# Two of four output blocks as seven block products, with their weight sums formed in DRAM

## The chip, the core and the metric

The kernel runs on one core of a Trainium2 chip. The metric is the device time of one execution in microseconds (us). Before the change the median of three runs is 1606.47 us (1606.38 to 1606.73). The core's engines work side by side: TensorE (PE) multiplies matrices, VectorE (DVE) and ScalarE (ACT) do elementwise work, GpSimd (POOL) a few small operations and accumulating DMA transfers, and SyncE (SP) issues the loads of the weights.

## The reference

One layer of a decoder trunk works on 256 rows of 2048 channels in float32: a normalisation, one wide projection `w_in`, a sparse attention branch and a retention branch, a gated merge of both, an output projection, and a squared-ReLU feed-forward part. What the change touches is the merge and what follows it:

```python
merged = jax.nn.sigmoid(ga) * (o_attn @ w_up_attn[l]) + jax.nn.sigmoid(gb) * (o_ret @ w_up_ret[l])
x = x + merged @ w_out[l]
h2 = rms_norm(x, ln2_g[l])
x = x + jnp.square(jax.nn.relu(h2 @ w_ff1[l])) @ w_ff2[l]
```

`merged`, `w_out`: 256 x 2048 and 2048 x 2048.

## The kernel before, in words

**Matmuls.** Each float32 operand is split into a rounded part hi and a rest lo, and a product is three matmuls, hi·hi, hi·lo and lo·hi (`products`, L434), of 128 x 128 stationary activations by 128 x 512 weights. The 256 rows are two row tiles t; the 2048 input channels are 16 k-chunks of 128. A *block* is 512 output columns: 16 chunks, 2 row tiles, 3 matmuls. The output projection has four blocks O0 to O3, the retention branch's projection UR0 to UR3, and the first group of the feed-forward part F1(1) and F1(0), in this order.

**Weights.** A load brings four chunks (1 MB) from DRAM into one of four buffers `raw` (L325 to L333) over SP's queue. Two chunks at a time, an *item*, are split: ScalarE writes `whi` (L379), VectorE `wlo` (L380). `program` (L150) lists all items in order; `ahead` (L397) issues loads up to 8 items and splits 2 items (3 from the feed-forward pools on) ahead of their use. Three pairs of split buffers go round, a fourth joins where the pool `f1` or `fourth` is there.

**Block products.** In the gates and in the later feed-forward groups two blocks together (2048 x 1024 weights, quarters A to D) are made by Strassen's scheme in Winograd's form: seven products of 8 chunks for one row tile each, in the order `ORDER`, in place of eight (`strassen`, L695). Some products use sums of quarters; VectorE adds those in the weight buffers (L367), and a few are added by an accumulating DMA of POOL into a buffer (L387). The products' banks are combined by VectorE (L712 to L724), with copies of three banks on ScalarE (L716). The activations need four differences (G3, G5, G6, G7) beside the plain quarters.

**Who sets the order.** The program text gives each instruction a place; a planner then places the instructions of each engine by a simulated time at which they are ready and, among those ready, by place. `tc.high_priority(offset=60)` puts an instruction 60 places ahead; in the gate stage the splits and the bank sums have it. Helpers such as norms and transposes are generators in a list `work`, advanced one `yield` by each `step()`, which is called once or twice per item.

**Around the change.** After UR0 and UR1, `merge` (L948) forms the merged rows on VectorE, `merged_in` (L944) transposes them on TensorE into a bank of the pool `pt` and splits them into `mT`. PSUM's eight banks are dealt as `pm` 4, `pt` 2, `pa` 2 there. After UR3 a `drain()` (L970) finishes all helpers. Then come O0 to O3 (L1029): each adds its bank into `x2` (L1033), squares it on ScalarE with a row sum (L1035) and writes it out to `sums`. After O2 the root of the mean square of three blocks is formed (L1040 to L1042, the power on POOL, L450), and the columns 0, 1 and 2 are normalised by it during O3 (`next_norm`, L988: a scaled copy L993, transposes L1001, a copy by the gain L1003, the split into `xf` L985 and L986). Column 3 follows in F1(1), with the differences for the block products (`forms`, L1009); a later factor makes up for the root of three blocks alone. F1(1) reads its chunks in the order of columns 0, 1, 2, 3.

Of the kernel before, what the change touches and what calls it, by code (L numbers as in the profile page):

```python
# [17 lines left out]
P = 128  # L18
# [60 lines left out]
def stream():  # L79
# [22 lines left out]
    b += [(("O", i), "w_out", 0, DK, i * BN, BN) for i in range(4)]  # L102
# [28 lines left out]
def block(key):  # L131

    return [(key, h, s) for h in range(DK // KC) for s in range(KC // HC)]
# [16 lines left out]
def program():  # L150
# [8 lines left out]
    for key in [("UR", 2), ("UR", 3)] + [("O", i) for i in range(4)] + [("F1", i) for i in (1, 0)]:  # L159
        out += block(key)  # L160
# [20 lines left out]
def block_kernel(ctx, tc, cst, rot, xt, gains, w, x, ret_gn_g, ret_gn_b, out):  # L181
# [89 lines left out]
    at, B, off = {}, {}, 0  # L271
    for key, name, _, nk, _, n in stream():
        B[key] = (nk, n)
        for h in range(nk // KC):
            src = w[off:off + KC * P * n].rearrange("(p c n) -> p c n", p=P, c=KC)
            if key in BESIDE:
# [5 lines left out]
    use = program()  # L282

    def tile_of(item):
        if item[0] == "Q":
# [5 lines left out]
    def sum_of(item):  # L291

        if item[0] == "Q":
# [57 lines left out]

    def split(i):
        if first_gate - 16 <= i <= last_gate:
# [43 lines left out]
    def ahead(i):  # L397
        for _ in range(2):
# [16 lines left out]
    def run_blocks(keys, act, before=None):  # L415
# [3 lines left out]
        for k0 in range(0, nk, HC):  # L419
            for key, p in zip(keys, ps):  # L420
                n = B[key][1]
                ws = weights((key, k0 // KC, k0 % KC // HC))
                for c in range(HC):
# [4 lines left out]
                    products(p, [z[:, c, :n] for z in ws], [act(k, t) for t in range(T)], k == 0, k == nk - 1)  # L428
        return [[z[:, :B[key][1]] for z in p] for key, p in zip(keys, ps)]

    def run_block(key, act, before=None):
        return run_blocks([key], act, before)[0]
# [262 lines left out]
    def strassen(item):  # L695
# [4 lines left out]
        p = ORDER[n]  # L700
# [12 lines left out]
        with tc.high_priority(offset=AHEAD) if u in GATES else nullcontext():  # L713
# [230 lines left out]
    def merged_in(i, t, m):  # L944
        yield from transpose_in(mT, 4 * i, t, m)
# [11 lines left out]
    for i in range(2):  # L957
        merge(i, both_ps[i])
    work.append(branches(2))
    for i in (2, 3):  # L960
        ps = run_block(("UR", i), of(rT))
        if i == 2:
            drain()
        merge(i, ps)
# [5 lines left out]
    drain()  # L970
    ex.release()
# [3 lines left out]
    late["f2"] = ctx.enter_context(tc.tile_pool(name="f2", bufs=1, side="right", reuse_waits="tile"))  # L975
# [3 lines left out]
    xf = late["f1"].tile([P, 2, len(PRODUCTS), HK, P], F32R, tag="xf", name="xf")  # L979
    xr = [late["f2"].tile([P, T, HK, P], F32, tag="rawb", name=nm("xr"), bufs=2) for _ in range(2)]  # L980
# [48 lines left out]
    for i in range(4):  # L1029
        ps = run_block(("O", i), of(mT))  # L1030
        for t in range(T):
            z = x2[:, t, i * BN:(i + 1) * BN]
            nc.vector.tensor_tensor(z, ps[t], z, op=ALU.add)  # L1033
            junk = stage()
            nc.scalar.activation(junk, z, AF.Square, accum_out=ss2[:, 4 * t + i:4 * t + i + 1])  # L1035
            nc.scalar.dma_start(sums[:, t, i * BN:(i + 1) * BN], z)
        if i == 2:

            ss = small(T)
            nc.vector.tensor_reduce(ss, ss2.rearrange("p (t i) -> p t i", t=T)[:, :, :3], axis=AX.X, op=ALU.add)  # L1040
            rs = cp.tile([P, T], F32, name="rs")
            nc.vector.tensor_copy(rs, rsqrt(ss, T, 1.0 / (3 * BN)))  # L1042
            work.append(z for k in range(3) for z in next_norm(k))
# [4 lines left out]
    def norm_end():  # L1048
        yield from next_norm(3)
# [24 lines left out]
    for i in (1, 0):  # L1074
        ps = run_block(("F1", i), lambda k, t: form(quads[k // HK][t], k % HK))
# [87 lines left out]
```

## Time and profile before

| what | us |
|---|---|
| median of three runs | 1606.47 |
| the profiled execution | 1606.29 |
| its span, first to last instruction | 1604.3 |
| TensorE busy in it | 1597.7 |
| VectorE busy | 1298.9 |
| ScalarE busy | 1017.4 |
| GpSimd busy | 126.5 |

In the rows of the profile, a line such as L380 is a line of the kernel, `out<-in` are the program's buffers, `xN` is a count. A row of instructions in order of time has the start, the busy time, the engine, the line and, in brackets, how long the engine stood idle ahead of it and who released it. A row of a stage has its bounds and length, then the busy time and number of instructions of TensorE, of its weight loads, of VectorE, ScalarE and GpSimd, then TensorE's granted clock, the busy share of the DMA engines and GB/s. A row of a group has the busy time, the mean in ns, and the idle time ahead. A row of waits has the total, the number and the longest. A row of transfers has the number, the size and the median time from issue to landing.

### The profile page before, as it was taken

Reading aid. Unit: us, or ns where it says so; the run is one execution under the profiler, and the core shown is the slowest. Engines: PE = TensorE matmul, PEld = TensorE weight load, DVE = VectorE, ACT = ScalarE, POOL = GpSimd, SP = SyncE. Lnnn points to the kernel's source line nnn. Section 1 sums busy time; section 2 is a strip of 40 time slices with the busy share of each in tenths; the row PEclk is TensorE's granted clock in tenths of the full one; section 3 lists DMA queues with packets and bytes.
Section 4 is the critical chain, followed back from the end, with each engine's and each line's share of the span. In section 5 each row is a group of like instructions: output and inputs, shape, how many; then the busy total and the mean of one; then the engine's idle time right before and its main releaser. Section 6 shows DMA issues by size and latency. Waiting matters only on the chain.

```text
span 1604.3 us, 19728 instructions
## 1 busy us (share of the span) xinstructions
PE 1597.7 (100%) x7394; PEld 1327.8 (83%) x7394; DVE 1298.9 (81%) x1354; ACT 1017.4 (63%) x1262; POOL 126.5 (8%) x169
## 2 busy tenths in 40 slices
PE   9999999999999999999999999999999999999998
PEld 8978888888888888888888888888888888888887
DVE  6578777998989899677765579898989898989884
ACT  7555567666766666454444666767767776767672
POOL 0000001010000001112210000000000000000000
PEclk9999999999999999999999999999999999999999
DMA  9645348978878684765766574767676767777673
GB/s 331 220 146 186 135 153 305 299 266 274 258 287 266 230 258 176 285 222 195 265 250 250 194 277 149 257 194 246 204 260 200 242 213 236 236 236 236 216 205 130
DMA packets 75759, 368.57 MB, mean 230 GB/s; under 512 B 8592, under 2 KB 15376, under 8 KB 42512
## 3 DMA queue, kind: packets, MB, share of 16 engines
q1 hardware_dynamic: 56224, 311.32, 53.0%
q0 software_dynamic: 16704, 49.82, 14.3%
q10 hardware_dynamic: 2736, 6.18, 1.0%
q8 instruction: 58, 0.95, 0.2%
q14 instruction: 37, 0.30, 0.1%
HBM read 337.92 MB, written 29.36 MB: 229 GB/s over the span
## 4 chain that ended last, share of the span: by engine, by line
PE 97%; DVE 2%; ACT 0%; issue 0%; DVEq 0%
PE pm L439 14%; PE pm L440 14%; PE pm L438 14%; PE pq L438 9%; PE pq L439 9%; PE pq L440 9%; PE pf L438 7%; PE pf L439 7%; PE pf L440 7%; PE pt L467 1%; DVE wlo L380 1%; DVE mid L593 1%; PE pa L438 0%; PE pa L439 0%; PE pa L440 0%; PE pa L264 0%
## 5 line engine op out<-in xcount | busy, mean ns | idle before, releaser
L380 DVE TENSOR_TENSOR wlo<-raw,whi 128x1024 fp32r<-128x1024 f32 (+2 forms) x556 | 659.7, 1200 | 206.1 <-ACT whi L379 197.9
L379 ACT ACTIVATE whi<-raw 128x1024 fp32r<-128x1024 f32 (+2 forms) x556 | 576.0, 1043 | 382.3 <-PE pm L440 233.9
L438 PE MATMUL pm<-whi,act 128*128 128x512 f32 (+1 forms) x992 | 384.7, 388 | 0.0
L439 PE MATMUL pm<-wlo,act 128*128 128x512 f32 (+1 forms) x992 | 381.8, 385 | 0.5 <-DVE wlo L380 0.5
L440 PE MATMUL pm<-whi,act 128*128 128x512 f32 (+1 forms) x992 | 381.4, 384 | 0.0
L380 DVE TENSOR_TENSOR wlo<-rawc,whi 128x1024 fp32r<-128x1024 f32 x176 | 214.7, 1220 | 42.2 <-ACT whi L379 40.4
L379 ACT ACTIVATE whi<-rawc 128x1024 fp32r<-128x1024 f32 x176 | 186.6, 1060 | 85.7 <-PE pf L440 23.2
L439 PEld LDWEIGHTS pm<-wlo,act 128*128 128x128 f32 x992 | 186.4, 188 | 35.9 <-DVE wlo L380 3.0
L440 PEld LDWEIGHTS pm<-whi,act 128*128 128x128 f32 x992 | 186.2, 188 | 35.1
L438 PEld LDWEIGHTS pm<-whi,act 128*128 128x128 f32 x992 | 186.4, 188 | 33.9 <-issue 0.3
L438 PE MATMUL pf<-whi,act 128*128 128x512 f32 x512 | 200.0, 391 | 0.0
L439 PE MATMUL pf<-wlo,act 128*128 128x512 f32 x512 | 199.4, 390 | 0.0
L440 PE MATMUL pf<-whi,act 128*128 128x512 f32 x512 | 199.4, 389 | 0.0
L367 DVE TENSOR_TENSOR raw<-raw,raw 128x2048 f32<-128x2048 f32 x86 | 196.6, 2286 | 0.8
L438 PE MATMUL pq<-whi,xf 128*128 128x512 f32 x392 | 154.3, 394 | 0.0
L439 PE MATMUL pq<-wlo,xf 128*128 128x512 f32 x392 | 152.8, 390 | 0.0
L440 PE MATMUL pq<-whi,xf 128*128 128x512 f32 x392 | 152.8, 390 | 0.0
L440 PEld LDWEIGHTS pf<-whi,act 128*128 128x128 f32 x512 | 96.1, 188 | 20.1
L438 PEld LDWEIGHTS pf<-whi,act 128*128 128x128 f32 x512 | 96.0, 188 | 20.1 <-ACT whi L379 0.4
L439 PEld LDWEIGHTS pf<-wlo,act 128*128 128x128 f32 x512 | 96.1, 188 | 19.7
L1109 POOL DMA_DIRECT2D sums<-ev x56 | 49.1, 969 | 580.8 <-ACT ev L1108 579.9
L440 PEld LDWEIGHTS pq<-whi,xf 128*128 128x128 f32 x392 | 73.6, 188 | 15.3
(206 smaller groups left out, 1623.2 us busy)
## 6 DMA issues: line engine op xcount, KB each, us to landing
raw<-in_w_dram SPq DMA_DIRECT2D x188, 1024.0 KB, 6.1
rawc<-in_w_dram SPq DMA_DIRECT2D x56, 1024.0 KB, 6.3
rawc<-in_w_dram SPq DMA_DIRECT2D x64, 512.0 KB, 5.9
sums<-ev POOLq DMA_DIRECT2D x56, 256.0 KB, 5.5
raw<-in_w_dram POOLq DMA_DIRECT2D x10, 1024.0 KB, 9.9
raw<-in_w_dram SPq DMA_DIRECT2D x8, 736.0 KB, 5.0
raw<-in_w_dram SPq DMA_DIRECT2D x7, 512.0 KB, 7.9
raw<-in_w_dram SPq DMA_DIRECT2D x8, 368.0 KB, 7.8
```

What stands on the lines that cost most here:

```text
L367: nc.vector.tensor_tensor(one, one, two, op=ALU.add)
L379: nc.scalar.activation(a, src, AF.Copy)
L380: nc.vector.tensor_tensor(b, src, a.bitcast(F32), op=ALU.subtract)
L438: nc.tensor.matmul(d, h, hi, start=first, stop=False, skip_group_check=skip)
L439: nc.tensor.matmul(d, h, lo, start=False, stop=False, skip_group_check=skip)
L440: nc.tensor.matmul(d, l, hi, start=False, stop=last, skip_group_check=skip)
L467: nc.tensor.transpose(ps[:, c * P:(c + 1) * P], src[:, c * P:(c + 1) * P], ident)
L593: nc.vector.scalar_tensor_tensor(sc[t], src, iw[:, t, h:h + 1], sc[t], op0=ALU.mult, op1=ALU.add)
L1109: nc.gpsimd.dma_start(sums[:, t, i * BN:(i + 1) * BN], z, accum_op=ALU.add)
```

## The change

The blocks O0 and O1 become one pair of block products, `OUT = ("O", 0)`, in the order X11 A, G7 B, X12 D, G5 A, G3 C, G6 C, X22 D. The sums of weight quarters that they need are formed in DRAM tiles `pre`: eight plain copies of 1 MB by SP at items 24 to 45, and eight accumulating transfers by POOL at items 46 to 73, all in the index and attention projections. The products' 14 loads and those of O2 and O3 go through the four `raw` buffers. The items of the first two products stand between those of UR3; then come four items of O2, and then the remaining 20 product items with the other 12 of O2 and O3 between them, the last of those ahead of the last three product items.

The splits of the stretch and the bank sums of `OUT` get the 60 places. `merged_in` also copies the transposed rows to `xr`, and a new helper `m_forms` makes the four differences. The banks are dealt as `pm` 4, `pq` 3, `pt` 1 right after UR0 and UR1; the drain after UR3 goes. The root for the norm is formed from the columns 2 and 1 alone, once both are complete; these two are normalised first, then 3 and 0, and F1(1) takes its chunks in that order.

```diff
+OUT = ("O", 0)
+OUT_ORDER = (0, 2, 5, 1, 3, 4, 6)
+NORM_COLS = (2, 1, 3, 0)
...
+def second_half():
+    q = [("Q", OUT, n, h, s) for n in range(len(OUT_ORDER)) for h in range(HK // KC) for s in range(KC // HC)]
+    a, b = q[:8], q[8:]
+    out = block(("UR", 2))
+    for x, y in zip(block(("UR", 3)), a):
+        out += [x, y]
+    two = block(("O", 2)) + block(("O", 3))
+    out, two = out + two[:4], two[4:]
+    n, j = len(b) - 2, 0
+    for i, x in enumerate(b):
+        out.append(x)
+        while j < len(two) and j * n < (i + 1) * len(two):
+            out.append(two[j])
+            j += 1
+    return out
...
+    pre = {z: dp.tile([HK // KC, P, KC * BN + 16], F32, name=nm("pre"))[:, :, :KC * BN].rearrange("h p (c n) -> h p c n", c=KC) for z in QUARTERS}
+    for n, p in enumerate(OUT_ORDER):
+        z = PRODUCTS[p][1]
+        for h in range(HK // KC):
+            at[("OQ", n), h] = (pre[z][h] if p in (1, 2, 4, 6) else base[z, h], BN)
+    background = {}
+    for j, (z, two) in enumerate((("A", "B"), ("B", "C"), ("C", "A"), ("D", "C"))):
+        for h in range(HK // KC):
+            background[24 + 6 * j + 3 * h] = (pre[z][h], base[z, h], False)
+            background[46 + 8 * j + 3 * h] = (pre[z][h], base[two, h] if j < 2 else pre[two][h], True)
...
     def split(i):
-        if first_gate - 16 <= i <= last_gate:
+        if first_gate - 16 <= i <= last_gate or first_out - 4 <= i <= last_out:
             with tc.high_priority(offset=AHEAD):
...
     def ahead(i):
+        if i in background:
+            d, a, add = background[i]
+            if add:
+                nc.gpsimd.dma_start(d, a, accum_op=ALU.add)
+            else:
+                nc.sync.dma_start(d, a)
...
-        with tc.high_priority(offset=AHEAD) if u in GATES else nullcontext():
+        with tc.high_priority(offset=AHEAD) if u in GATES or u == OUT else nullcontext():
...
     def merged_in(i, t, m):
...
+        split_into(mT, 4 * i, 4, t, ps)
+        half, c0 = divmod(4 * i, HK)
+        nc.scalar.activation(xr[half][:, t, c0:c0 + 4, :], ps.rearrange("p (c i) -> p c i", c=4), AF.Copy)
         moved[0] += 1
...
+    deal(pm=4, pq=3, pt=1)
...
+    def m_forms():
+        while moved[0] < 2 * T:
+            yield
+        for c in (0, 4):
...
+            nc.vector.tensor_tensor(d, xr[0][:, 1, c:c + 4, :], xr[0][:, 0, c:c + 4, :], op=ALU.subtract)
+            nc.scalar.activation(hi, d, AF.Copy)
...
+            nc.vector.tensor_tensor(lo, d, hi.bitcast(F32), op=ALU.subtract)
...
+        for f, d, one, two in ((G5, x22, x21, x22), (G6, x11, x11, x22), (G3, x12, x12, x11)):
...
+    def out_block(i, t, src):
+        z = x2[:, t, i * BN:(i + 1) * BN]
+        nc.vector.tensor_tensor(z, src, z, op=ALU.add)
+        junk = stage()
+        nc.scalar.activation(junk, z, AF.Square, accum_out=ss2[:, 4 * t + i:4 * t + i + 1])
+        nc.scalar.dma_start(sums[:, t, i * BN:(i + 1) * BN], z)
+        done.add((i, t))
...
-    drain()
-    ex.release()
...
+    def first_norms():
+        lo, n = min(NORM_COLS[:2]), 2
+        ss = small(T)
+        nc.vector.tensor_reduce(ss, ss2.rearrange("p (t i) -> p t i", t=T)[:, :, lo:lo + n], axis=AX.X, op=ALU.add)
+        nc.vector.tensor_copy(rs, rsqrt(ss, T, 1.0 / (n * BN)))
+        for k in NORM_COLS[:2]:
+            yield from next_norm(k)
...
+        if not started and all((i, t) in done for i in NORM_COLS[:2] for t in range(T)):
+            started = True
+            work.append(first_norms())
     drain()
...
-        yield from next_norm(3)
+        for k in NORM_COLS[2:]:
+            yield from next_norm(k)
...
-        ps = run_block(("F1", i), lambda k, t: form(quads[k // HK][t], k % HK))
+        ps = run_block(("F1", i), lambda k, t: form(quads[k // HK][t], k % HK), order=NORM_COLS if i else range(DK // KC))
```

More of the change, by code (lines that the diff above doesn't have):

```diff
@@ L699, in strassen @@
         b, e = blocks[u]["b"], blocks[u]["e"]
-        p = ORDER[n]
+        p = product_of(u, n)
         ws = weights(item)
@@ new lines, in m_forms @@
+    def m_forms():
+        while moved[0] < 2 * T:
+            yield
+        for c in (0, 4):
+            z = stage()
+            d = z.rearrange("p (c i) -> p c i", c=4)
+            hi, lo = m7[c // KC] = [sp.tile([P, KC, P], F32R, tag="stg", name=nm("stg"), bufs=n_stg) for _ in range(2)]
+            nc.vector.tensor_tensor(d, xr[0][:, 1, c:c + 4, :], xr[0][:, 0, c:c + 4, :], op=ALU.subtract)
+            nc.scalar.activation(hi, d, AF.Copy)
+            yield
+            nc.vector.tensor_tensor(lo, d, hi.bitcast(F32), op=ALU.subtract)
+            yield
+        while moved[0] < 4 * T:
+            yield
+        (x11, x21), (x12, x22) = ([z[:, t] for t in range(T)] for z in xr)
+        for f, d, one, two in ((G5, x22, x21, x22), (G6, x11, x11, x22), (G3, x12, x12, x11)):
+            hi, lo = (mx["xf"][:, a, f] for a in range(2))
+            nc.vector.tensor_tensor(d, one, two, op=ALU.subtract)
+            nc.scalar.activation(hi, d, AF.Copy)
+            yield
+            nc.vector.tensor_tensor(lo, d, hi.bitcast(F32), op=ALU.subtract)
+            formed.add(f)
+            yield
@@ new lines, in plain @@
+    def plain(item, act):
+        (key, i), h, s = item
+        ws = weights(item)
+        if (h, s) == (0, 0):
+            acc[key, i] = [psum("pm") for _ in range(T)]
+        for c in range(HC):
+            step()
+            k = h * KC + s * HC + c
+            products(acc[key, i], [z[:, c] for z in ws], [act(k, t) for t in range(T)], k == 0, k == DK - 1)
+        return acc.pop((key, i)) if k == DK - 1 else None
+    done = set()
+    def out_block(i, t, src):
[5 more added lines that the diff above has]
+        done.add((i, t))
@@ new lines, in block_kernel @@
+    work.append(branches(2))
+    work.append(m_forms())
+    blocks[OUT] = {"form": m_form, "finish": lambda u, t, i, dst, src: out_block(i, t, src), "b": {}, "e": {}}
+    rest = second_half()
+    while rest[0][0] != ("O", 2):
+        item = rest.pop(0)
+        if item[0] == "Q":
+            strassen(item)
+            continue
+        ps = plain(item, of(rT))
+        if ps:
+            if item[0][1] == 2:
+                while moved[0] < T * 2 or any(z.gi_frame is not None and z.__name__ == "branches" for z in work):
+                    step()
+            merge(item[0][1], ps)
@@ L1027, in forms @@
         late["g7"] = xr[0][:, 1:2]
[L1029 to L1043, printed above, removed]
+    rs = cp.tile([P, T], F32, name="rs")
+    def first_norms():
[5 more added lines that the diff above has]
+            yield from next_norm(k)
+    started = False
+    while rest:
+        item = rest.pop(0)
+        if item[0] == "Q":
+            strassen(item)
+        else:
+            ps = plain(item, of(mT))
+            for t in range(T if ps else 0):
+                out_block(item[0][1], t, ps[t])
+        if not started and all((i, t) in done for i in NORM_COLS[:2] for t in range(T)):
+            started = True
+            work.append(first_norms())
     drain()
```

65 lines of the change are left out of this document (43 added, 22 removed).

## The prediction

> **What bounds the kernel now.** I read the page first, for busy times and for the chain that ended last.
>
> ```profile
> PE 1597.7 (100%) x7394; PEld 1327.8 (83%) x7394; DVE 1298.9 (81%) x1354; ACT 1017.4 (63%) x1262; POOL 126.5 (8%) x169
> ...
> PE 97%; DVE 2%; ACT 0%; issue 0%; DVEq 0%
> ```
>
> A busy TensorE need not be a TensorE at its peak, since ends are modelled. So the second view is the list of what TensorE waited for, and the third its instructions one by one in a plain output block (the first and the last of 54 matmuls).
>
> ```profile
> PE pa L264 <- DVE warm L259: 1.1, 1, 1.1
> PE pq L438 <- ACT mid L676: 0.9, 1, 0.9
> PE pm L439 <- DVE wlo L380: 0.5, 2, 0.3
> ```
> ```profile
> 879.82 0.39 PE L439 MATMUL pm<-wlo,act 128*128 128x512 f32 x1
> ...
> 891.83 0.39 PE L438 MATMUL pm<-whi,act 128*128 128x512 f32 x1
> ```
>
> TensorE waits 2.5 us in the whole run, and one matmul of 512 columns follows the other every (891.83 - 879.82) / 53 = 0.2266 us. The kernel is bound by its number of matmuls: one less is worth 0.2266 us, as long as nothing new makes TensorE wait. All the rest of the argument is about new waits. The profiled execution took 1606.29 us (span 1604.3 and 2.0 around it), 0.18 under the median 1606.47 of the three runs; the sum is made on 1606.29, and 0.18 is added at the end.
>
> **Matmuls removed.** Two plain output blocks are 2 x 16 k-chunks x 2 row tiles x 3 = 192 matmuls. Seven products of 8 k-chunks x 3 are 168. The transposes keep their number. 24 x 0.2266 = **-5.44 us**. This is all that can be won.
>
> **Splits, forms, bank sums and copies added.** 28 weight splits stand in place of 16, and there are four differences of activations with their splits, five bank sums, three bank copies and eight copies of transposed rows. These rows give what the engines do now from the third UR block to late in the last O block, in the gate stage (which already runs such products beside plain blocks), in the 22 us in which three columns are normalised, and in the 22 us at the start of the output blocks; then the price of one split (VectorE's half) and of one sum.
>
> ```profile
> 812.00:924.00 112.00, 112.00 (x514) 92.59 (x513) 63.19 (x67) 58.91 (x81) 0.72 (x1) 1.00 0.61 223
> 250.00:500.00 250.00, 250.00 (x1103) 206.29 (x1102) 224.09 (x188) 173.61 (x192) 22.62 (x37) 1.00 0.84 284
> 902.00:924.00 22.00, 22.00 (x109) 18.04 (x108) 12.70 (x17) 18.48 (x33) 0.72 (x1) 1.00 0.47 161
> 836.00:858.00 22.00, 22.00 (x100) 18.30 (x100) 13.36 (x14) 9.84 (x11) 0.00 (x0) 1.00 0.81 319
> ```
> ```profile
> L380 DVE TENSOR_TENSOR wlo<-raw,whi 128x1024 fp32r<-128x1024 f32 (+2 forms) x556 | 659.7, 1200 | 206.1 <-ACT whi L379 197.9
> ```
> ```profile
> 333.43 0.68 DVE L712 TENSOR_TENSOR stg<-pq,stg 128x512 f32<-128x512 f32 x1
> ...
> 335.17 1.29 DVE L712 TENSOR_TENSOR stg<-stg,stg 128x512 f32<-128x512 f32 x2
> 336.37 0.68 DVE L712 TENSOR_TENSOR stg<-pq,stg 128x512 f32<-128x512 f32 x1
> 336.97 1.21 DVE L380 TENSOR_TENSOR wlo<-raw,whi 128x1024 fp32r<-128x1024 f32 x1
> ...
> 344.85 0.74 DVE L785 SCALAR_TENSOR_TENSOR stg<-stg,r,stg 128x512 f32<-128x512 f32 x1
> ```
>
> VectorE gets 12 x 1.20 for splits, four ops of 0.68 and six of about 1.2 for the differences, and 5 x 0.68 for sums: 14.4 + 10 + 3.4 = 28. 63 + 28 = 91 us of 112 - 5 = 107, or 85%. The gate stage has 224 / 250 = 90% and TensorE waits nowhere in it. ScalarE gets 12 x 1.04 (a row of its own chain further down), and eleven copies and five activation splits between 0.6 and 1.05, some 11 us: 59 + 24 = 83 of 107, or 77%; the row at 902 has 18.5 / 22 = 84%, again without a wait. So this work costs 0, its cover being matmuls at a load that other stages carry. Its upper end is 1 us, about the one wait of 0.9 above.
>
> **One transpose bank where there were two.** A bank of transposed rows is read by three operations, hi, lo and the new copy, 0.6 to 0.7 each. Were two sets of transposes queued back to back on the one bank, TensorE, in order, would stand about 1.9 us, and all matmuls behind it; four such pairs are 7.6. The feed-forward stage has the same deal of banks:
>
> ```profile
> 1114.47 0.49 PE pt L467 x4
> 1117.04 0.44 PE pt L467 x4
> ```
>
> There the two sets stand 2.6 us apart, matmuls between them, with no entry in the list of waits. I take 0 of the range 0 to 7.6. The drain after the last UR block goes too; its transposes are covered by the four items of O2 that follow, 48 x 0.2266 = 10.9 us.
>
> **The memory sums.** Eight plain copies of 1 MB stand in SP's queue ahead of weight loads, and eight accumulating transfers in POOL's, between some 60 and 190 us. No row has a transfer from memory to memory; the nearest are weight loads of 1 MB in that stretch and the gate stage's accumulation into a buffer (POOL's queue); the third row is SP's longest wait, that for a split to free a buffer.
>
> ```profile
> raw<-in_w_dram SPq DMA_DIRECT2D x10, 1024.0 KB, 4.8
> ```
> ```profile
> raw<-in_w_dram POOLq DMA_DIRECT2D x7, 1024.0 KB, 10.2
> ```
> ```profile
> SPq L333 <- DVE wlo L380: 1091.5, 239, 16.1
> ```
>
> So one is 4.8 to 10.2 us of transfer. There are four weight buffers, and a plain block uses up one in 24 x 0.2266 = 5.44 us; a load that finds one copy ahead lands 10 to 15 us after its issue, against three further buffers, 16.3 us. It fits: 0. Two transfers ahead of one load would miss by up to 4.8 + 2 x 10.2 - 16.3 = 9 us: the upper end, and a rival below. Behind a POOL transfer stands only the small power of a norm in that stretch, about an issue (0.5 to 1 us) late.
>
> **The norm behind the output blocks: where I expect the loss.** Now the root of three blocks' squares is formed while the fourth block (96 matmuls, 21.8 us) runs. These rows, VectorE's and then ScalarE's in order of time, are the chain from the last matmul of the third block.
>
> ```profile
> 899.71 1.28 DVE L1033 TENSOR_TENSOR x<-pm,x 128x512 f32<-128x512 f32 x2
> ...
> 902.51 0.16 DVE L1040 TENSOR_REDUCE small<-ss 128x2 f32<-128x6 f32 x1
> ...
> 903.71 0.17 DVE L1042 COPY rs<-small 128x2 f32<-128x2 f32 x1 [0.84 <-POOL small L450]
> ...
> 908.81 1.29 DVE L986 TENSOR_TENSOR xf<-xr,xf 128x512 fp32r<-128x512 f32 x2 [1.35 <-ACT xf L985]
> ...
> 914.44 1.29 DVE L986 TENSOR_TENSOR xf<-xr,xf 128x512 fp32r<-128x512 f32 x2
> ```
> ```profile
> 903.91 1.34 ACT L993 ACTIVATE stg<-x,rs 128x512 f32<-128x512 f32 x2 [1.44 <-DVE rs L1042]
> 905.16 1.04 ACT L379 ACTIVATE whi<-raw 128x1024 fp32r<-128x1024 f32 x1
> 906.11 1.54 ACT L1003 ACTIVATE xr<-pt,gT 128x256 f32<-128x256 f32 x4
> ```
>
> From the block's end to the first half column that a matmul can use (908.81 + 0.68) it is 9.8 us, with 12 us to spare. After the change the root needs columns 2 and 1, and column 1 is complete with product G6 C, the sixth. Behind that stand four items of the seventh product (6 matmuls each) and two of O3 (12 each): 48 x 0.2266 = 10.9 us, and the first column's own eight transposes, some 0.9 (four took 0.44 above). Cover: **11.8 us**. Then F1 needs column 2 and TensorE has nothing else to do.
>
> The chain gets longer. Ahead of it come four bank sums, 0.60 apart: 2.4. They and the splits up to the last product are 60 places ahead in priority, the adds into x2 are not, so the second add can fall behind the splits of the next three items, 3 x 1.14 = 3.4; the gate rows show it happen, the sums until 336.97 and the ordinary operation behind them at 344.85, behind splits. The one bank makes the two halves of a column follow one another: up to 0.7. Least: 9.8 + 2.4, without the 1.0 that another split took on ScalarE in the old chain, 11.2: hidden. Most: 9.8 + 2.4 + 3.4 + 0.7 = 16.3, a wait of 4.5, and 5.5 with one more split on ScalarE. I take two of the three splits and half of the bank's share, nearest to the gate rows: 9.8 + 2.4 + 2.3 + 0.4 = 14.9. **+3.1 us.** What is late next is column 1, then 3 and 0; the old columns came 914.44 - 908.81 = 5.6 us apart, and F1 uses one up in 24 x 0.2266 = 5.4 and 0.9 of transposes, so the wait doesn't grow.
>
> Sum: 1606.29 - 5.44 + 3.1 = 1603.95, and with 0.18 **1604.1 us**.
>
> **The rivals.** *The chain is hidden*: the second add is placed ahead of the splits. For it: VectorE has no raw sums left in this stretch (the gate stage has them) and is some 60% loaded behind the differences. Against: the priorities. Wait 0 to 2: 1601.0 to 1603.1.
>
> *The products' weights come late* (the slower side). From the last UR block to the end of O3 26 loads of 1.05 MB, 2.1 of x and 2.1 of sums, 31.5 MB, fall on 456 x 0.2266 = 103.3 us: 305 GB/s, through four buffers, where the gate stage has more. At the gate stage's 284 GB/s it takes 110.9: +7.6, so 1604.1 + 7.6 = 1611.7. It decides from 299 GB/s down (the gain gone), and is slower than can be told below 290. Against it: 319 GB/s at a share of 0.81 in the row at 836, without a wait.
>
> *The memory sums hold up a weight load* once or twice early on: up to +9, 1604.1 to 1613, most likely 1607.
>
> *The array restarts slowly after the wait.* By the profile's clock row (1.00 in every row above) no wait of the old kernel, 1.1 us at most, cost any clock. A wait of 3 to 5.5 is longer than any it shows; at half the rate for as long as the warming at the start of the chain lasts, 5.7 us, it would cost 2.8: 1606.9.
>
> ```profile
> 1.06 5.70 PE pa L264 x28
> ```
>
> [...]
>
> **How the numbers follow.** The wait of 2 to 5.5 us: 0.46, its own range 1603.1 to 1606.5. Hidden: 0.32. Weights late: 0.10. Memory sums: 0.07. Slow restart: 0.05. A difference of 0.2%, 3.2 us, is about what can be told from none; faster by more is below 1603.3. Hidden and a little of the first make 0.36 faster; most of the first, the restart and half of the memory sums 0.50 the same; the rest, 0.14, slower. The range leaves out the late weights, the worse memory sums and the last half us of the hidden case: 1601.3 to 1608.
>
> **What would show it.** 24 fewer matmuls, at 0.2266. A new entry in the list of TensorE's waits, at F1's first matmuls, behind ScalarE or VectorE writing xf, of 2 to 5 us, and the adds into x2 between splits. Under 2 us there: hidden. ScalarE's splits waiting for DMA in the stretch: the second rival. TensorE waiting between 60 and 200 us, or for pt: the memory sums, the bank. I am wrong if TensorE waits anywhere else for more than 1 us, or if the chain is short.

## The result, and the profile after

The changed kernel takes 1622.37 us (median of five runs, 1621.14 to 1623.05) against 1606.47: a ratio of 1.0098 [1.0083, 1.0112], slower by 15.9 us. The profiled execution took 1621.14, its span is 1619.2 against 1604.3.

The page of the kernel after, its busy times and the shares of the chain that ended last:

```profile
PE 1599.9 (99%) x7370; PEld 1326.3 (82%) x7370; DVE 1326.8 (82%) x1381; ACT 1039.4 (64%) x1290; POOL 131.4 (8%) x177
...
PE 92%; DVE 3%; DMA 3%; ACT 1%; issue 1%; POOL 0%; DVEq 0%; ACTq 0%
```

The 24 matmuls are gone (7394 to 7370), and still TensorE is busy for 2.2 us longer. Busy time doesn't show a gain or a loss here, since a matmul that runs slowly counts as busy (0.63 us in the rows of F1's start below, where the usual one has 0.39). The new thing is in the chain: 3% of the span, some 49 us by that rounded share, now pass through DMA, where before there was none.

What TensorE waited for in the kernel after (in total, times, longest):

```profile
PE pm L492 <- ACT whi L426: 5.2, 3, 2.5
PE pm L493 <- DVE wlo L427: 2.5, 5, 0.8
PE pt L1130 <- ACT xr L1132: 1.9, 2, 0.9
PE pt L1130 <- ACT stg L1122: 1.8, 2, 1.6
...
PE pm L492 <- ACT xf L1114: 0.7, 1, 0.7
PE pt L1003 <- ACT xr L1006: 0.6, 2, 0.4
```

There are two groups: splits of weights (7.7 us, 7.4 of them between 40 and 160 us; L426 and L427 are the split), and the norm at the start of F1 (L1114 to L1132, 4.4 us). To see where each lies, I put two events of all kernels beside each other: the start of ScalarE's first copy of a bank in the gate stage, and the start of its first read of F1(1)'s finished bank.

| kernel | first gate bank | F1(1)'s bank | between | span |
|---|---|---|---|---|
| before | 290.90 | 946.90 | 656.0 | 1604.3 |
| after | 301.05 | 961.64 | 660.6 | 1619.2 |

So 10.2 us are lost ahead of 291, in the projections where the memory sums are formed and where the change leaves the matmuls as they were, and 4.6 between the two events, where 5.4 should have been won. Behind F1(1) nothing changes (657.6 against 657.4 to the end of the span). The two losses make up the 14.9 us by which the spans differ; the profiled execution was the fastest of the five.

**The first loss.** Two stages of 20 us, kernel after and then kernel before (length, busy times and counts of TensorE, its loads, VectorE, ScalarE and GpSimd, granted clock, DMA share, GB/s):

```profile
60.00:80.00 20.00, 17.64 (x105) 17.09 (x104) 7.68 (x9) 8.66 (x11) 0.82 (x1) 1.00 1.02 308
...
120.00:140.00 20.00, 15.13 (x60) 10.76 (x60) 14.48 (x50) 4.95 (x6) 1.63 (x2) 0.99 1.02 317
```
```profile
60.00:80.00 20.00, 20.00 (x120) 19.60 (x119) 10.00 (x12) 11.01 (x15) 0.00 (x0) 1.00 0.70 245
...
120.00:140.00 20.00, 20.00 (x87) 15.65 (x86) 18.22 (x51) 9.84 (x12) 1.64 (x1) 1.00 0.62 213
```

The DMA engines are full (1.02) at only some 310 GB/s, and TensorE stands. The transfers from 40 to 160 us, by queue (packets, MB, share of 16 engines) and by issue, of the kernel after and then of the kernel before:

```profile
q1 hardware_dynamic: 6421, 28.66, 61.6%
q0 software_dynamic: 1152, 8.39, 34.2%
...
raw<-in_w_dram SPq DMA_DIRECT2D x16, 1024.0 KB, 16.1
pre<-in_w_dram SPq DMA_DIRECT2D x8, 1024.0 KB, 18.3
pre<-in_w_dram POOLq DMA_DIRECT2D x4, 1024.0 KB, 12.3
pre<-pre POOLq DMA_DIRECT2D x4, 1024.0 KB, 13.7
```
```profile
q1 hardware_dynamic: 5475, 21.90, 52.9%
...
raw<-in_w_dram SPq DMA_DIRECT2D x17, 1024.0 KB, 4.8
```

All eight accumulating transfers (queue q0) lie in this stretch: 34.2% of 120 us is 41 us of all 16 engines, 5.1 us each. The last of them is issued at 135.55 us. A weight load now lands 16.1 us after its issue in the median and 27.1 at the longest, not 4.8, where the prediction had three further buffers last 16.3. ScalarE's splits waited 25.4 us for such loads in these 120 us (six waits; in the kernel before none), and TensorE waited for the splits. Behind the longest of its waits, 2.53 us, the granted clock was 0.50 for 3.41 us (rows in the last section), which adds at most half of that.

**The second loss.** VectorE of the kernel after, from the last matmul of G6 C (it starts at 917.01) on, to its half of the split of xf at the end of the chain. L766 are bank sums, L427 splits, L1077 the adds into x2, L1164 the sum for the root:

```profile
918.32 0.68 DVE L766 TENSOR_TENSOR stg<-pq,stg 128x512 f32<-128x512 f32 x1
918.92 1.22 DVE L427 TENSOR_TENSOR wlo<-raw,whi 128x1024 fp32r<-128x1024 f32 x1
920.05 1.29 DVE L766 TENSOR_TENSOR stg<-stg,stg 128x512 f32<-128x512 f32 x2
...
921.85 2.35 DVE L427 TENSOR_TENSOR wlo<-raw,whi 128x1024 fp32r<-128x1024 f32 x2
924.12 1.29 DVE L1077 TENSOR_TENSOR x<-stg,x 128x512 f32<-128x512 f32 x2
925.32 1.29 DVE L1077 TENSOR_TENSOR x<-pm,x 128x512 f32<-128x512 f32 x2
926.52 1.22 DVE L427 TENSOR_TENSOR wlo<-raw,whi 128x1024 fp32r<-128x1024 f32 x1
927.65 0.16 DVE L1164 TENSOR_REDUCE small<-ss 128x2 f32<-128x4 f32 x1
...
935.08 1.29 DVE L1115 TENSOR_TENSOR xf<-xr,xf 128x512 fp32r<-128x512 f32 x2 [4.73 <-ACT xf L1114]
```

And TensorE, from the last matmul of the products:

```profile
927.89 0.39 PE L494 MATMUL pq<-whi,act 128*128 128x512 f32 x1
929.83 0.33 PE L1130 MATMUL pt<-csb,stg 128*128 128x128 f32 x1 [1.55 <-ACT stg L1122]
...
931.92 1.11 PE L1130 MATMUL pt<-csb,stg 128*128 128x128 f32 x4 [0.93 <-ACT xr L1132]
...
935.10 0.80 PE L492 MATMUL pm<-whi,xf 128*128 128x512 f32 x1
935.69 0.63 PE L493 MATMUL pm<-wlo,xf 128*128 128x512 f32 x1
936.12 0.63 PE L492 MATMUL pm<-whi,xf 128*128 128x512 f32 x1
```

From 927.89 + 0.23 to 935.10 no weight is multiplied: 7.0 us. The matmuls then follow one another in 0.43 us (935.69, 936.12), twice the usual 0.2267, and the granted clock of the stage says the same (0.83):

```profile
920.00:940.00 20.00, 16.30 (x66) 12.38 (x65) 11.95 (x19) 13.86 (x27) 0.71 (x1) 0.83 0.65 211
```

### The profile page after: what moved, and what is told of

Same layout as the page of the kernel before. It is cut to its first block, busy times and chain, and to the rows that moved or that the text cites. A ratio compares the mean times of both kernels' runs of the same rounds, so it can differ in the third digit from the quotient of the medians.

```text
span 1619.2 us, 19791 instructions
## 1 busy us (share of the span) xinstructions
PE 1599.9 (99%) x7370; PEld 1326.3 (82%) x7370; DVE 1326.8 (82%) x1381; ACT 1039.4 (64%) x1290; POOL 131.4 (8%) x177
## 4 chain that ended last, share of the span: by engine, by line
PE 92%; DVE 3%; DMA 3%; ACT 1%; issue 1%; POOL 0%; DVEq 0%; ACTq 0%
PE pm L493 12%; PE pm L494 12%; PE pm L492 12%; PE pq L492 10%; PE pq L494 10%; PE pq L493 10%; PE pf L492 7%; PE pf L494 7%; PE pf L493 7%; DMA raw<-in_w_dram 3%; DVE wlo L427 1%; PE pt L521 1%; ACT whi L426 1%; PE pa L492 0%; PE pa L493 0%
## 5 line engine op out<-in xcount | busy, mean ns | idle before, releaser
L427 DVE TENSOR_TENSOR wlo<-raw,whi 128x1024 fp32r<-128x1024 f32 (+2 forms) x568 | 676.3, 1207 | 188.3 <-ACT whi L426 177.5
L426 ACT ACTIVATE whi<-raw 128x1024 fp32r<-128x1024 f32 (+2 forms) x568 | 588.3, 1043 | 372.3 <-PE pm L494 188.1
L492 PE MATMUL pm<-whi,act 128*128 128x512 f32 (+1 forms) x928 | 360.4, 389 | 5.2 <-ACT whi L426 5.2
L493 PE MATMUL pm<-wlo,act 128*128 128x512 f32 (+1 forms) x928 | 357.6, 385 | 2.5 <-DVE wlo L427 2.5
L494 PE MATMUL pm<-whi,act 128*128 128x512 f32 (+1 forms) x928 | 357.2, 385 | 0.0
L427 DVE TENSOR_TENSOR wlo<-rawc,whi 128x1024 fp32r<-128x1024 f32 x176 | 215.1, 1222 | 41.8 <-ACT whi L426 40.0
L426 ACT ACTIVATE whi<-rawc 128x1024 fp32r<-128x1024 f32 x176 | 186.5, 1060 | 85.3 <-PE pf L494 23.3
L492 PEld LDWEIGHTS pm<-whi,act 128*128 128x128 f32 x928 | 174.7, 188 | 37.7 <-ACT whi L426 6.7
L493 PEld LDWEIGHTS pm<-wlo,act 128*128 128x128 f32 x928 | 174.9, 188 | 35.9 <-DVE wlo L427 5.1
L494 PEld LDWEIGHTS pm<-whi,act 128*128 128x128 f32 x928 | 174.7, 188 | 32.8
L492 PE MATMUL pq<-whi,xf 128*128 128x512 f32 x416 | 163.8, 394 | 0.2 <-ACT stg L770 0.2
L493 PE MATMUL pq<-wlo,xf 128*128 128x512 f32 x416 | 162.1, 390 | 0.0
L494 PE MATMUL pq<-whi,xf 128*128 128x512 f32 x416 | 162.1, 390 | 0.0
L494 PEld LDWEIGHTS pq<-whi,xf 128*128 128x128 f32 x416 | 78.1, 188 | 16.3
```

The lines of the kernel that those rows point to most:

```text
L426: nc.scalar.activation(a, src, AF.Copy)
L427: nc.vector.tensor_tensor(b, src, a.bitcast(F32), op=ALU.subtract)
L492: nc.tensor.matmul(d, h, hi, start=first, stop=False, skip_group_check=skip)
L493: nc.tensor.matmul(d, h, lo, start=False, stop=False, skip_group_check=skip)
L494: nc.tensor.matmul(d, l, hi, start=False, stop=last, skip_group_check=skip)
```

## The experiments

The theory is that two things cost the time, apart from each other: the memory sums fill the DMA engines in the first 140 us, and the norm's chain is not covered at the start of F1, with a slow restart of the array behind it. The rivals: the copies alone, by standing ahead of loads in SP's queue; ScalarE and VectorE being too full for the norm wherever it stands; a wait that costs only itself. Each time is a median, with the kernel before, measured beside it (1606.69 to 1607.16), as the base of the ratio.

**The sums.** In `no_sums` both kinds of transfers are left out (the edit shown), in `copies_only` the accumulating ones alone (the last of its removed lines).

```diff
-            at[("OQ", n), h] = (pre[z][h] if p in (1, 2, 4, 6) else base[z, h], BN)
+            at[("OQ", n), h] = (base[z, h], BN)
-            background[24 + 6 * j + 3 * h] = (pre[z][h], base[z, h], False)
-            background[46 + 8 * j + 3 * h] = (pre[z][h], base[two, h] if j < 2 else pre[two][h], True)
```

> No sum is formed in memory: the eight copies and the eight accumulating transfers are left out, and the products read plain quarters in place of the sums, so the output blocks 0 and 1 come out wrong; all else is as after. Theory A (the sums fill the DMA engines early on, loads come late, TensorE waits): the start of the gates moves back by all 10.2 us, so 1622.4 - 10.2 = 1612.2, no wait of TensorE between 60 and 150 us, the clock 1.00 there, and the wait at F1 stays at 7 us. Rival B (the planner's other order of the early stage costs it, and the transfers only happen to be there): no gain over 2 us, above 1620.

> The eight plain copies in SP's queue stay, the eight accumulating transfers in POOL's are left out (the products read copies of plain quarters, so the output blocks 0 and 1 come out wrong). Theory A, by engine time: the accumulating queue held the engines for 34% of 120 us, 41 us, the copies some 21; with the copies alone the share between 60 and 140 us falls from 1.02 to about 0.7 and the loads land within 10 us: 1612 to 1614. Rival C (the copies stand ahead of the weight loads in SP's queue, and that is what makes them late, not the engines' total): most of the 10.2 us stays, 1619 to 1622.

Measured: `no_sums` 1611.64, 1.0031 [1.0019, 1.0042], and its first gate bank starts at 291.00, as in the kernel before, while the wait at F1 stays, at 6.9 us: the two losses are separate. `copies_only` 1612.02, 1.0031 [1.0020, 1.0043], 291.19. So the copies by themselves cost nothing that can be told, and the accumulating transfers, together with the copies, the whole first loss of 10 us. The transfers of `copies_only` from 40 to 160 us:

```profile
q1 hardware_dynamic: 6659, 30.22, 70.1%
...
raw<-in_w_dram SPq DMA_DIRECT2D x17, 1024.0 KB, 5.2
pre<-in_w_dram SPq DMA_DIRECT2D x8, 1024.0 KB, 9.8
```

Eight copies are (70.1 - 52.9)% of 120 us, 20.6 us of all engines, 2.6 each: an accumulating transfer of the same size took 5.1, twice that.

Is it the amount or the crowd? `paced` keeps all sixteen transfers and spreads them: a pair at every eighth item from 20 to 76, the copy tied behind the weight load issued last.

```diff
-            background[24 + 6 * j + 3 * h] = (pre[z][h], base[z, h], False)
-            background[46 + 8 * j + 3 * h] = (pre[z][h], base[two, h] if j < 2 else pre[two][h], True)
+            background[20 + 8 * (2 * j + h)] = (pre[z][h], base[z, h], False)
+            background[20 + 8 * (2 * j + h) + 1] = (pre[z][h], base[two, h] if j < 2 else pre[two][h], True)
...
-                nc.sync.dma_start(d, a)
+                with tc.issue_after(last_load[0].ins):
+                    nc.sync.dma_start(d, a)
```

> All sums are formed, output complete; only the moment changes: each of the eight copies is tied in SP's queue behind the weight load of an item, eight items apart (20, 28, ... 76), so one copy follows every four loads and one accumulating transfer follows each copy. Theory A (62 us of engine time squeezed into the 85 us from 50 to 135 us, beside loads that need half of it): over some 175 us the share stays near 0.5 + 62/175 = 0.85, loads land in under 10 us, TensorE doesn't wait, and it comes to the time without sums, 1611.6 to 1613. Rival F (an accumulating transfer itself slows the loads beside it, whenever it comes): 8 such transfers still cost, above 1617.

Measured: 1611.50, 1.0029 [1.0018, 1.0041]; first gate bank 290.78. The same sums, issued up to 233 us instead of 136, cost nothing. The transfers of `paced`, from 40 to 160 us, and its accumulations in the whole run (duration of an issue, first and last start):

```profile
raw<-in_w_dram SPq DMA_DIRECT2D x17, 1024.0 KB, 6.7
...
pre<-in_w_dram POOLq DMA_DIRECT2D x4, 1024.0 KB, 8.4
```
```profile
L448 POOL DMA_DIRECT2D pre<-pre x4: 872/876/880, 144.9 to 233.1; - x4
```

**The norm.** In `root_one` the root comes from column 2 alone, which is complete earlier, and the norm of the next column starts by itself; `no_sums_root_one` is the same without the memory sums.

```diff
-        lo, n = min(NORM_COLS[:2]), 2
+        lo, n = NORM_COLS[0], 1
...
-        for k in NORM_COLS[:2]:
-            yield from next_norm(k)
+        yield from next_norm(NORM_COLS[0])
...
+        for n, z in enumerate((first_norms, lambda: next_norm(NORM_COLS[1]))):
+            if started == n and all((NORM_COLS[n], t) in done for t in range(T)):
+                started = n + 1
+                work.append(z())
+                break
```

> The sums as in the kernel after; the root for the norm is formed from column 2 alone, as soon as O2 is complete, and column 1 is normalised when it is complete. Theory D (the wait at F1's start is the chain from the sixth product over sums, root and column 2, and the slow clock follows from that wait): the 7 us wait and the 1.4 us of slow matmuls behind it go, the granted clock is 1.00 there, 1622.4 - 8.5 = 1613.9. Rival E (ScalarE can't normalise columns at the rate at which F1 uses them up, so the wait moves to a later column): gain under 4 us, above 1618.

> Both edits: no sums in memory (output blocks 0 and 1 wrong) and the root from column 2 alone. If A and D hold and add up, what is left is the 24 matmuls saved, 5.4 us, less small waits of 1 to 2 us: 1601 to 1603. If either cause is another, above 1606.

Measured: 1619.16 (four runs, from 1617.52 to 1621.08), 1.0077 [1.0062, 1.0092], and 1609.03, 1.0013 [1.0004, 1.0022]: 3.2 and 2.6 us won of the second loss, where theory D put 8.5. Both lie where the rivals had put them. TensorE in `no_sums_root_one`, where F1 begins at once and then stops for a weight split that stands behind the next column's norm on ScalarE:

```profile
925.64 0.73 PE L491 MATMUL pm<-whi,xf 128*128 128x512 f32 x2 [1.87 <-ACT whi L425]
926.90 0.50 PE L492 MATMUL pm<-wlo,xf 128*128 128x512 f32 x1 [0.53 <-DVE wlo L426]
...
928.45 0.63 PE L492 MATMUL pm<-wlo,xf 128*128 128x512 f32 x1
928.88 0.63 PE L493 MATMUL pm<-whi,xf 128*128 128x512 f32 x1
```

The wait has moved, and again matmuls 0.43 us apart follow it. `no_sums_ahead` takes another way: root from two columns as in the change, but the adds and squares of column 1 and the root have 120 places.

```diff
+        with tc.high_priority(offset=2 * AHEAD) if i == 1 else nullcontext():
+            out_rows(i, t, src)
...
+        with tc.high_priority(offset=2 * AHEAD):
+            ss = small(T)
```

> As without the sums (output blocks 0 and 1 wrong), with the adds into x2 and the squares of block 1 and the root's few operations placed 120 ahead, so ahead of the weight splits. Theory I (the wait at F1's start is set by these operations standing behind splits on VectorE): the adds start 2.3 us earlier, the reduce 1.7 more, the wait falls from 7.0 to 3 to 4 us, and with less idle time the slow clock goes: 1611.6 - 4 = 1607.5 or so. Rival J (the chain is mostly latency of its ten steps, and ScalarE's order sets it): the wait stays over 5.5, above 1610.

Measured: 1610.12, 1.0019 [1.0010, 1.0028], 1.5 under `no_sums`; a wait of 4.9 us at F1 is left (its first matmul at 923.76, the last product matmul ended at about 918.9), more than theory I put and less than rival J: the chain is still longer than what is behind column 1. `paced_root_splits` combines the pacing, the root from column 2 and 60 places for the splits of F1's first block:

```diff
-        if first_gate - 16 <= i <= last_gate or first_out - 4 <= i <= last_out:
+        if first_gate - 16 <= i <= last_gate or first_out - 4 <= i <= last_out + 8:
```

> All of the output is computed. The copies paced as in the first, the root from column 2 alone, and the weight splits of F1's first block placed 60 ahead as well, since with the root from one column TensorE stood 2.4 us at F1's second item for a split that was queued on ScalarE behind the copies of column 1. If A, D and this reading are right, the waits left are those of single splits and transposes, 2 us: 1606.6 - 5.4 + 2 = 1603.2. If the paced sums still cost or column 1 is late instead, 1606 to 1610.

Measured: 1610.16, 1.0018 [1.0009, 1.0027], just above the rival's range. What TensorE waits for in it:

```profile
PE pt L1131 <- ACT stg L1123: 1.6, 1, 1.6
...
PE pt L1131 <- ACT xr L1133: 0.9, 1, 0.9
```

These waits are at 935 to 937, for column 3: with the splits ahead, the norm of the later columns is late. So whichever of the two goes first on ScalarE, the other is late, as long as both must happen at the start of F1.

`no_sums_fill` was meant to keep the array busy during the wait with small matmuls on zeros (6 ahead of the drain, 4 behind each of column 2's two sets of transposes), to see whether the half rate goes.

```diff
+    def idle(n):
+        ps = psum("pq")
+        for _ in range(n):
+            nc.tensor.matmul(ps[:, :P], warm, warm, start=True, stop=True)
+        nc.vector.tensor_copy(small(8), ps[:, :8])
```

> As without the sums (output blocks 0 and 1 wrong), and 14 calls of a small matmul on zeros into a spare bank are put into the wait at F1's start, 6 ahead of it and 4 after each set of transposes of column 2. Theory G (the matmuls behind the wait run at 0.43 us because the array stood idle): with the fill the granted clock stays near 1.00 there, the first matmuls of F1 follow one another at 0.227, and 1.5 us come back, 1610.1, though the wait for column 2 itself stays. Rival H (they are slow for another reason, such as ScalarE and VectorE working on the same buffers): still 0.43, 1611.6 or a little more.

Measured: 1613.96, 1.0043 [1.0029, 1.0057], 2.3 slower than `no_sums`. Part of the filler ran early, inside O3 (at 910.45), the waits between the sets of transposes stayed (0.33, 1.29 and 1.25 us), and the matmuls were again 0.43 apart, until 933.1. The filler did not fill the wait, so this run tells nothing of the restart.

**A wait in the kernel before.** `before_root_late` is the kernel before with one edit: the root from all four columns, so that nothing covers the chain.

```diff
-        if i == 2:
+        if i == 3:
-            nc.vector.tensor_reduce(ss, ss2.rearrange("p (t i) -> p t i", t=T)[:, :, :3], axis=AX.X, op=ALU.add)
+            nc.vector.tensor_reduce(ss, ss2.rearrange("p (t i) -> p t i", t=T)[:, :, :4], axis=AX.X, op=ALU.add)
-            nc.vector.tensor_copy(rs, rsqrt(ss, T, 1.0 / (3 * BN)))
+            nc.vector.tensor_copy(rs, rsqrt(ss, T, 1.0 / (4 * BN)))
```

> The kernel before with one edit: the root is formed from all four columns, behind O3, so no matmul is left to cover the chain of 9.8 us from a block's last matmul to F1's first half column (the computation is whole). Nothing else of the change is in it. If a wait costs only itself: 1606.5 + 8.9 to 10 = 1615.4 to 1616.5, matmuls at 0.2266 us right behind it. If the array restarts slowly: the matmuls behind the wait 0.43 us apart for 3 to 6 us, 1.5 to 3 us more, 1617 to 1619.5, granted clock of that stretch near 0.83.

Measured: 1614.92, 1.0049 [1.0034, 1.0064], 7.8 us. TensorE behind its last output matmul, which starts at 921.64:

```profile
926.57 2.16 PE L1001 MATMUL pt<-csb,stg 128*128 128x128 f32 x8 [4.54 <-ACT stg L993]
...
932.00 0.63 PE L438 MATMUL pm<-whi,xf 128*128 128x512 f32 x1
932.42 0.63 PE L440 MATMUL pm<-whi,xf 128*128 128x512 f32 x1
```

The half rate, and a granted clock of 0.83 from 920 to 940 us, came with a plain wait too, without anything of the change. The total, 7.8, is below the 8.9 to 10 that I had put for the wait alone, since the sixteen transposes in it are work, not wait, and I had counted them as wait. Most of the slow stretch falls on them (eight in 2.16 us; in the kernel before four took 0.44). The size of the restart is read from the rows, not from the total: the first five gaps between matmuls, from 930.98 to 933.28, are 2.3 us in place of 1.13, so 1.2 us.

**The order and the cover.** If the norm's work cannot be done at the start of F1, it must be spread. In `paced_early`, `paced_early_one` and `paced_early4` the plain items of O2 and O3 end earlier, and the columns go in the order 2, 3, 1, 0, so that the two late ones, 1 and 0, have half a block of F1 as cover. The first edit is that of `paced_early`; `paced_early_one` adds the root from column 2 alone; `paced_early4` has 4 in place of 8.

```diff
-NORM_COLS = (2, 1, 3, 0)
+NORM_COLS = (2, 3, 1, 0)
...
-    n, j = len(b) - 2, 0
+    n, j = len(b) - 8, 0
```

> The whole computation, with the memory sums paced as in the paced kernel; new: the plain items of O2 and O3 end eight product items ahead of the last one (they ended three ahead), the root comes from the columns 2 and 3, which are normalised first, and F1 reads the columns in the order 2, 3, 1, 0. Cover theory (the wait at F1 is a chain with too little TensorE work behind it): behind O3 now stand 8 x 6 x 0.2266 = 10.9 us of product matmuls, and the late column 1 has F1's 10.9 us on the columns 2 and 3; waits at F1 under 1.5 us, matmuls not at half rate, time some 6 under the paced kernel's 1611.5: 1604 to 1607. Rival (ScalarE and VectorE cannot carry splits, bank sums and the norm together in this stretch, wherever the norm stands): the wait of 2 to 5 us moves, to the splits of the last products or to the columns 1 and 0 in F1, again with 0.43-us matmuls behind it: 1608 to 1612.

> The whole computation; as paced_early, with the root from column 2 alone, which is complete a block's 12 items or more ahead of the end of the products. Cover theory: nothing more is won than by paced_early where that has no wait left (1604 to 1607); where paced_early still waits at F1's first column, this one does not. Rival: columns 1 and 0 are late in F1 in any case, 1608 to 1612.

> The whole computation; as paced_early, but O2 and O3 end only four product items ahead of the last. Cover theory: cover is 4 x 6 x 0.2266 = 5.4 us and some 0.9 of transposes, against a chain of 11 to 15 from O3's last matmul: a wait of 5 to 8 with half rate behind it, 1609 to 1612, some 4 or more above paced_early. Rival: the same time as paced_early within 1.5 us, since the load of the two engines is the same.

Measured: `paced_early` 1609.84, 1.0014 [1.0005, 1.0024]; `paced_early_one` 1606.13, 0.9994 [0.9985, 1.0003]; `paced_early4` 1611.05, 1.0024 [1.0015, 1.0034]. I missed the first: 10.9 us of cover behind O3 were not enough for a root that waits for two columns. The third lies 1.2 us above the first, where the cover theory put 4 or more and the rival under 1.5, so these two runs alone speak for the rival: half the cover made little difference. The second decides between them, by the earlier root, with the same work for both engines: the granted clock is 1.00 again in all of F1's start, and only single waits are left. That refutes the rival by which the two engines cannot carry the norm in this stretch at all. What counted was when the chain could start, more than how much matmul work stood behind O3.

**What was left.** `paced_early_one` still waited for its one transpose bank (L1004, 1.2 us) and for F1's first split (1.45 us). `early_one_bank` gives the three readers of the bank the 60 places; `early_one_all` gives them to F1's first two items' splits too; `early6_one_all` is that with 6 in place of 8.

```diff
-        split_into(mT, 4 * i, 4, t, ps)
         half, c0 = divmod(4 * i, HK)
-        nc.scalar.activation(xr[half][:, t, c0:c0 + 4, :], ps.rearrange("p (c i) -> p c i", c=4), AF.Copy)
+        with tc.high_priority(offset=AHEAD):
+            split_into(mT, 4 * i, 4, t, ps)
+            nc.scalar.activation(xr[half][:, t, c0:c0 + 4, :], ps.rearrange("p (c i) -> p c i", c=4), AF.Copy)
```

> The whole computation; paced_early_one with one edit: the three readers of the transposed rows in the one bank (hi, lo, the copy) have the 60 places, like the splits. Bank theory: the waits of the transposes (1.2 us in the list, 1.7 with their stagger at 790 to 820 us) go, under 0.3 left: 1606.1 - 1.3 = 1604.8. Rival: the readers push a split back, and the matmuls wait for that instead: 1606 or more.

> The whole computation; early_one_bank with the 60 places for the splits of F1's first two items too, which stand behind the last bank sums and adds (a wait of 1.45 us for a wlo at 923.8). If these two are what was left: lost cadence of 780 to 960 down from 5.8 to about 2.5, 1606.1 - 1.3 - 1.5 = 1603.3, under the kernel before by some 3. Rival (as in paced_root_splits, F1's splits ahead push the norm of the later columns back): a new wait of 1 to 3 us for the columns 1 or 0 in F1, 1605 to 1608.

> The whole computation; early_one_all with O2 and O3 ending six product items ahead of the last, not eight: cover behind O3 6 x 6 x 0.2266 = 8.2 in place of 10.9 us, and fewer products in a row that take a split of VectorE (1.20 us) every 1.36 us. If the root from column 2 alone makes the cover ample: within 0.7 us of early_one_all. If O3's own norm (column 3, second in F1) needs it: a wait of 1 to 3 us at column 3, 1605 to 1607.

Measured: `early_one_bank` 1604.11, 0.9985 [0.9976, 0.9993]; `early_one_all` 1605.06, 0.9990 [0.9982, 0.9999]; `early6_one_all` 1604.92, 0.9989 [0.9980, 0.9998]. The first is 2.6 us under the kernel before (1.1 to 3.9 by its interval), and 18 under the changed one. What TensorE waited for in it:

```profile
PE pm L494 <- DVE wlo L427: 2.2, 4, 1.5
...
PE pt L1004 <- ACT xr L1008: 0.8, 2, 0.7
```

In the second, the wait for F1's first split went and one for column 1 came (0.8 for xf and 0.6 for its bank), as the rival said. The third lies within 0.2 us of the second, so with the early root 8.2 us of cover do as well as 10.9. The two events of the table above, for the kernels on which this account rests:

| kernel | first gate bank | F1(1)'s bank | between | span |
|---|---|---|---|---|
| no_sums | 291.00 | 951.87 | 660.9 | 1609.3 |
| paced | 290.78 | 951.87 | 661.1 | 1609.5 |
| no_sums_root_one | 291.14 | 949.25 | 658.1 | 1606.7 |
| paced_early_one | 291.29 | 947.08 | 655.8 | 1604.5 |
| early_one_bank | 290.78 | 944.96 | 654.2 | 1602.5 |
| before_root_late | 291.18 | 955.37 | 664.2 | 1612.6 |

By 656.0 of the kernel before, `early_one_bank` wins 1.8 of the 5.4 us in this one trace. The other 3.6 are waits: of the 2.2 above 1.8 fall between the two events, and the 0.8 do, where the kernel before waited 0.3; that leaves some 1.3 in gaps that the list of waits doesn't name.

## Why the prediction was wrong

- **Matmuls, -5.44.** Right: 24 fewer, 0.2267 us apart (917.01 and 927.89 are 48 matmuls, 10.88 us). The gain is real, but the best kernel shows only 1.8 of it between the two events, and 2.6 in its median.
- **Splits, forms, bank sums, 0.** Right for the stretch as a whole, with room: I had put VectorE at 85% and ScalarE at 77% of it, and they are at 82.36 / 107 = 77% and 65.33 / 107 = 61%, as this stage of the kernel after shows (the same work as from 812 on before, 10.2 us later). But the average says nothing of the last 10 us, where the order decides: from 918 to 928 VectorE is busy for 9.97 of 10.00, and the adds and the root of the norm stand in that queue.

```profile
822.00:929.00 107.00, 105.74 (x472) 86.67 (x471) 82.36 (x84) 65.33 (x75) 2.79 (x3) 1.00 0.79 284
```

- **One transpose bank, 0 of 0 to 7.6.** Small, but not 0: 0.6 us of waits at L1003 in the kernel after, 1.2 in `paced_early_one`. Giving the bank's readers priority brought some 1.5 (1604.11 against 1606.13, with kernels before that differ by 0.5; 1.6 between the two events), though the two intervals overlap.
- **The memory sums, 0, with an upper end of 9.** This is the step that failed first: 10.2 us. Its reasoning went by one load and one copy ahead of it, and three things in it were wrong. It took the transfers to be spread over 60 to 190 us, as the item numbers say; but the planner places an instruction when it is ready, which the description of the kernel before said, and GpSimd had nothing else to do, so the accumulations were issued behind their copies, from 56.5 to 135.6 us. It priced a transfer by its time to landing and never by what it takes of the 16 engines: 8 x (5.1 + 2.6) = 62 us of all of them. And it never asked what was free: from 52 to 154 us, where the engines are full in the kernel after (1.02), they are busy for 0.52 of the time in the kernel before, which leaves some 49 us for these 62. Over the 130 us that I had assumed, 60 to 190, the share is 0.49 and leaves 66: the price alone would have fitted, the spreading did not happen. `paced` shows that over twice the time there is room. The rival "the memory sums hold up a weight load" had the right place and the right kind of loss, but with one or two late loads in mind, a chance of 0.07 and a most likely time of 1607.
- **The norm, +3.1 of 0 to 5.5.** The mechanism was right, the size not: a wait of 7.0. From the last matmul's end, 917.24, to the first half of xf, 935.08 + 0.68, it is 18.5 us, not 14.9. The sums and splits ahead of the adds took 6.9 (to 924.12) where I had 4.7: sums and splits alternate, and the sums do not go first. From the adds to the root it was 3.5, not the old 2.8: O3's two adds and one more split stand in front of the sum for the root. From the root on it was 8.1, not 7.0 and the 0.4 allowed for the bank: the scaled copies share ScalarE with O3's squares, and the transposes one bank. The cover is 10.9, since the 0.9 of transposes that I had counted into it come inside the wait. F1's first matmul needs only hi and starts 0.7 ahead of the 18.5, at 935.10, which gives the 7.0.
- **The rivals.** *Hidden* (0.32) and *weights late* (0.10) fall: between 780 and 960 us no split waits for a transfer. *Slow restart* (0.05) came true beside the others, not in place of them; from 935.10 to 938.33 the weights' matmuls ran at half rate, some 1.6 us lost, where I had put 2.8, for an assumed 5.7 us at half rate. I had made cases exclusive that add up: the memory sums at 1607 and the restart at 1606.9 are 2.9 and 2.8 above 1604.1, and both together, 1609.8, lay outside the range.
- **What would show it.** The signs that I named were the right ones (TensorE waiting between 60 and 200 us; a wait at F1's first matmuls; the adds between splits), each larger than put.

## What to carry to other kernels

Transfers that are added beside a full stream of loads are to be priced in time of all DMA engines, against what the stream leaves free in the very stretch where they will be issued (here 62 us against 49); and where a planner places what is ready, a later place in the program does not delay a transfer, only a dependency does. A plan that shortens TensorE's work has to look at what its last product releases: how long the chain behind that is, how much matmul work covers it and, above all here, when it can start. Order and cover together brought 1.7 us (`paced` to `paced_early`), the root from one column another 3.7, a priority 1.5 to 2.0 at most. The order alone was not tested. A wait of TensorE could cost more than itself here, 1.2 us more behind the 4.54 of `before_root_late`, so cases in which TensorE stops are to be added up, not weighed against each other.

## What was unexpected of the hardware

An accumulating transfer from memory to memory took 5.1 us of all 16 engines per MB in the kernel after, and 5.5 in `paced` (22.8% of 120 us for five). A plain copy took 2.6 in `copies_only`; this is a difference of two shares, and by the same way it is 1.8 in `paced` (60.4% against 52.9% for five), with which the 62 us above would be 55. While both ran beside the loads, the engines were full at 308 to 361 GB/s of traffic.

The half rate did not begin with the first matmul behind a wait. In the kernel after, early on, one matmul took 0.49 us after 2.53 us of waiting, and only behind another 0.77 us came the slow ones, 0.43 us apart:

```profile
138.76 0.49 PE L492 MATMUL pm<-whi,act 128*128 128x512 f32 x1 [2.53 <-ACT whi L426]
140.02 0.80 PE L493 MATMUL pm<-wlo,act 128*128 128x512 f32 x1 [0.77 <-DVE wlo L427]
140.61 0.63 PE L494 MATMUL pm<-whi,act 128*128 128x512 f32 x1
141.04 0.63 PE L492 MATMUL pm<-whi,act 128*128 128x512 f32 x1
```

In `no_sums_root_one`, behind waits of 1.87 and 0.53 us, the matmuls from 927.23 to 927.69 still followed one another in 0.23 us, and from 928.02 on, 2.4 us after the work had resumed, in 0.43. Here are two neighbouring stretches of the kernel after, the idle one, at a granted clock of 1.00, and the one behind it, at 0.50, as rows of a stage:

```profile
136.19:139.61 3.42, 0.53 (x2) 0.19 (x1) 0.87 (x1) 1.96 (x3) 0.17 (x1) 1.00 1.06 434
139.61:143.02 3.41, 3.00 (x7) 2.44 (x8) 3.38 (x7) 3.18 (x6) 0.00 (x0) 0.50 1.01 271
```

TensorE was busy for 0.53 of 3.42 us in the first, and the matmul at 138.76 still belongs to it. Waits of nearly the same length did not have the same end. Behind 1.84 and 0.52 us, at 75 us in the kernel after, the matmuls (of 368 columns there) followed one another in the usual 0.17 us from 76.98 on; behind 1.87 and 0.41 us at the same place in `root_one`, in 0.31 us from 77.12 to 79.27. No run varied a wait alone, so what decides between the two is not shown.
